# Modulation weights at the head of SyncE's queue, small loads on ScalarE, and a one-column root refined on ScalarE

## The chip, the cores and the metric

The kernel runs on one core of a Trainium2 chip. The metric is device time in microseconds (us) of one launch. "Before" is the median of three runs; a separate profiled execution gives the trace.

## What is computed

Two layers (DEPTH = 2) of a backbone over 2048 latent tokens and 256 context tokens, 1024 wide, all in float32. Cut to what matters here:

```
mod_x = silu(c) @ w_ada[l] + b_ada[l]            # shift, scale, gate for the latent tokens
mod_c = silu(c_ctx) @ w_ada[l] + b_ada[l]        # the same for the context tokens
hx = x * rsqrt(mean(x*x) + EPS) * g_pre * (1 + sc_x) + sh_x
px = hx @ w_in[l]                                # columns for four head groups
# mLSTM, Hyena (FFT convolution with a filter made by a small sine MLP), gated linear attention, windowed attention
y = concat(groups) @ w_out[l]
x = x + gt_x * (y * rsqrt(mean(y*y) + EPS) * g_post)
```

The context tokens go the same way with `mod_c`. The filter of the Hyena group is `sin(f1 * (z @ w1 + b1))`, then `sin(f2 * (h @ w2 + b2))`, then a third matrix product.

## The kernel before

Tokens are handled in 18 tiles of 128: two context tiles, then 16 latent tiles. A scheduler of the language orders the instructions of every engine when the program is built, by its own model of durations; each engine then runs its list strictly in that order. All DMA transfers stand in one list, on SyncE (SP).

The start of the program (`start`, L393) does five things that overlap. `ada_prep` (L233) loads 72 short rows (`rows`: the two conditioning vectors, biases, `g_pre`, the sine frequencies), TensorE transposes them, and `fm` and `cs` come out of it. `hy_mlps` (L238 to L1285) is the sine MLP of the filter: per block of up to 512 columns a product (L1265), a scaled copy on ScalarE (`sa`, L1230), five VectorE instructions that reduce the argument (L1231 to L1235), a sine on ScalarE (L1236), and all that once more for the second layer (product at L1271). The sine is in another ScalarE function table than the logarithm and exponential, so a table is loaded ahead of the sines and another after the last one (L1284); the logarithm of every normalisation is tied behind the latter. `ada_first` (L314) loads 16 tiles of the modulation weights, 512 KB each, and multiplies them (L266); from the sums come `A` and `B`, scale and shift per feature. `phase_a` (L382) loads token tiles (`cvhi`, `cvho`, `xh`) and calls `norm_tile` (L349): a Square with a running sum on ScalarE (L360), the inverse root (`rsqrt_mean`), a scaling on VectorE (L364), transposes on TensorE (L370), scale and shift (L374, L377), and a split into a rounded part `hi` (L379) and a remainder `lo`, written `ho` in the rows (L380, GpSimd). Then `weights` (L411) loads and splits the projection weights (`raw`, two buffers; `w`), and the projection itself runs at L480 to L483. Between these runs the rest of the filter (`hy_spectrum`; L1342 to L1350, L1390, L1404).

`rsqrt_mean` (L220) takes a sum of squares `ss` of one column (`nss` in `norm_tile`, `rs` at the end of a layer; 36 and 34 calls) or of four (the head norms; 68 calls). It forms v = mean + EPS on VectorE, Ln and Exp(-0.5 ...) on ScalarE, and one Newton step in three VectorE instructions (L228 to L230).

A layer ends with `tail` (L1605): per tile, the mLSTM chunk (`mlstm_chunk`: decay matrices `E` loaded by L798, L804 to L828 on VectorE, products L810 and L816), the output projection (L1650 to L1652), its norm (L1653 to L1659) and the residual (L1660). Tiles overlap, two or three at a time.

Of the kernel before, what the change touches and what calls it, by code (L numbers as in the profile page):

```python
# [18 lines left out]
P = 128  # L19
D = 1024  # L20
# [136 lines left out]
class Net:  # L157
    def __init__(self, ctx, tc, a):
        self.tc, self.nc, self.a = tc, tc.nc, a
        nc = self.nc  # L160
        pool = lambda name, bufs=1, **kw: ctx.enter_context(tc.tile_pool(name=name, bufs=bufs, **kw))
        nc.scalar.preload_act_table_set("natural_log_exp_and_others")
        self.dram = pool("dram", space=DRAM)
        self.cst = pool("cst")
        self.hp = pool("hp")
        self.wp = pool("wp")
        self.gp = pool("gp")
        self.psp = pool("psp", 2, space=PSUM)
        self.psm = None
        self.nd = 0  # L170
        self.marks, self.pacer = [], None
        self.flip = 0
        self.H2, self.KX, self.KC = {}, {}, None
        self.rev = [1, 0] + list(range(NT - 1, NCT - 1, -1))
        self.ident = self.cst.tile([P, P], F32, name="ident")
        nc.sync.dma_start(out=self.ident, in_=a["c_ident"])
        self.aT = self.dt((NT, P, KD, P), "aT")
# [42 lines left out]
    def rsqrt_mean(self, p, ss, n, tag):  # L220
# [6 lines left out]
        nc.scalar.activation(out=ss, in_=t, func=ACTF.Exp, scale=-0.5)  # L227
        nc.vector.scalar_tensor_tensor(out=t, in0=ss, scalar=-0.5, in1=ss, op0=ALU.mult, op1=ALU.mult)  # L228
# [4 lines left out]
    def ada_prep(self, p):  # L233
        nc, a = self.nc, self.a
        rows = p.tile([64 + 4 * DEPTH, P], F32, name="rows")
        nc.sync.dma_start(out=rows[0:8], in_=a["c"].rearrange("o (k p) -> (o k) p", p=P))
        nc.sync.dma_start(out=rows[8:16], in_=a["c_ctx"].rearrange("(k p) -> k p", p=P))
        for h in range(2):  # L238
            o, c = 64, slice(64 * h, 64 * h + 64)
            nc.sync.dma_start(out=rows[o:o + 2 * DEPTH, c], in_=a["hyena_freq"].rearrange("l j p -> (l j) p"))  # L240
            for j, nm in enumerate(("hyena_b1", "hyena_b2")):
                r = o + (2 + j) * DEPTH
                nc.sync.dma_start(out=rows[r:r + DEPTH, c], in_=a[nm])
        for l in range(DEPTH):
            o = 16 + 24 * l
            nc.sync.dma_start(out=rows[o:o + 16], in_=a["b_ada"][l, :2 * D].rearrange("(k p) -> k p", p=P))
            nc.sync.dma_start(out=rows[o + 16:o + 24], in_=a["g_pre"][l].rearrange("(k p) -> k p", p=P))
# [65 lines left out]

    def ada_first(self):  # L314
        nc = self.nc
        ws = [self.hp.tile([P, 4, D], F32, tag=t, name="ws" + t, bufs=4) for t in ("hi", "ho") * 2]
        slots = [ws[i // 4][:, i % 4] for i in range(16)]

        def load(l, k, u):
            w = slots[u * KD + k]  # L320
            nc.sync.dma_start(out=w, in_=self.a["w_ada"][l, k * P:(k + 1) * P, u * D:u * D + D])
            return [w[:, 256 * q:256 * q + 256] for q in range(4)]
# [70 lines left out]
    def start(self, src):  # L393
        self.pa_banks = ("ab",)
        self.ev = (3,)
        with self.banks("st"):
            with self.pool("ad0", 1) as pa:
                self.ada_prep(pa)
# [839 lines left out]
    def hy_mlps(self, layers, banked=False):  # L1238
        nc, a = self.nc, self.a
        nl = len(layers)  # L1240
        with self.banks("hm") if banked else nullcontext(), self.pool("hm", LG[13]) as p:
# [4 lines left out]
            ls = slice(layers[0], layers[-1] + 1)  # L1246
            for h in range(2):
                r = slice(64 * h, 64 * h + 64)
                nc.sync.dma_start(out=W1[33 * h:33 * h + 33, :, r], in_=a["hyena_w1"][ls].rearrange("l p n -> p l n"))
                nc.sync.dma_start(out=W2[r, :, r], in_=a["hyena_w2"][ls].rearrange("l p n -> p l n"))  # L1250
            zs = {}
            for nm, n in (("x", SEQ // 2), ("c", CTX))[:1 if layers[0] else 2]:
                zs[nm] = p.tile([66, n], F32, name="z" + nm, bufs=1)
                nc.sync.dma_start(out=zs[nm], in_=a["c_z" + nm])
# [494 lines left out]
```

## Time and profile before

| quantity | value |
|---|---|
| median of three runs | 3533.69 us (3526.88 to 3543.3) |
| the profiled execution: its own time | 3536.89 us |
| its span, first to last instruction | 3535.1 us |
| mean granted TensorE clock | 0.944 |
| TensorE (PE) busy | 3226.2 us, 91% |
| VectorE (DVE) busy | 2046.1 us, 58% |
| ScalarE (ACT) busy | 1434.5 us, 41% |
| GpSimd (POOL) busy | 1153.3 us, 33% |

The span is the part of the profiled execution that the trace covers, 1.8 us less than its time. The busy shares are means over stages with different limits, so a stage is read from its own stretch of the trace.

### The profile page before, as it was taken

Reading aid. Unit: us, or ns where it says so; the run is one execution under the profiler, and the core shown is the slowest. Engines: PE = TensorE matmul, PEld = TensorE weight load, DVE = VectorE, ACT = ScalarE, POOL = GpSimd, SP = SyncE. Lnnn points to the kernel's source line nnn. Section 1 sums busy time; section 2 is a strip of 40 time slices with the busy share of each in tenths; the row PEclk is TensorE's granted clock in tenths of the full one; section 3 lists DMA queues with packets and bytes.
Section 4 is the critical chain, followed back from the end, with each engine's and each line's share of the span. In section 5 each row is a group of like instructions: output and inputs, shape, how many; then the busy total and the mean of one; then the engine's idle time right before and its main releaser. Section 6 shows DMA issues by size and latency. Waiting matters only on the chain. (4 is left out here: it accounts for less than half of the span.)

```text
span 3535.1 us, 70724 instructions
## 1 busy us (share of the span) xinstructions
PE 3226.2 (91%) x25897; PEld 2653.8 (75%) x25897; DVE 2046.1 (58%) x5374; ACT 1434.5 (41%) x3722; POOL 1153.3 (33%) x1559
## 2 busy tenths in 40 slices
PE   6989999999998988888998899998999999887998
PEld 4778878798886677777777677776888887776776
DVE  6733565553345565568888534656432457745887
ACT  5513444332544444133444323444333546522433
POOL 3711111233123344145555420112231135422555
PEclk8999999999998989989999899999999999998999
DMA  7374443684355532475444365443863443327453
GB/s 248 105 203 125 116 117 101 186 247 130 111 167 155 149 111 82 120 203 176 154 138 137 97 178 156 118 116 118 242 185 97 123 119 105 101 84 210 152 162 106
DMA packets 554861, 508.24 MB, mean 144 GB/s; under 512 B 114896, under 2 KB 484877, under 8 KB 554515
## 3 DMA queue, kind: packets, MB, share of 16 engines
q1 hardware_dynamic: 554515, 503.73, 48.3%
q8 instruction: 205, 3.36, 0.4%
q14 instruction: 141, 1.16, 0.1%
HBM read 337.64 MB, written 165.92 MB: 142 GB/s over the span
## 5 line engine op out<-in xcount | busy, mean ns | idle before, releaser
L480 PE MATMUL pp<-w,hi 128*128 128x256 f32 (+2 forms) x1984 | 602.8, 305 | 23.6 <-ACT w L425 10.4
L482 PE MATMUL pp<-w,hi 128*128 128x256 f32 (+2 forms) x1984 | 595.6, 301 | 4.5 <-POOL w L426 4.5
L483 PE MATMUL pp<-w,ho 128*128 128x256 f32 (+2 forms) x1984 | 590.8, 298 | 5.1 <-POOL ho L380 5.0
L463 PE MATMUL pp<-hi,w 128*128 128x512 f32 (+1 forms) x1328 | 527.0, 397 | 6.5 <-ACT w L425 5.2
L466 PE MATMUL pp<-hi,w 128*128 128x512 f32 (+1 forms) x1328 | 513.6, 389 | 1.2 <-POOL w L426 1.0
L465 PE MATMUL pp<-ho,w 128*128 128x512 f32 (+1 forms) x1328 | 513.6, 387 | 0.0
L480 PEld LDWEIGHTS pp<-w,hi 128*128 128x128 f32 x1984 | 389.3, 197 | 46.4 <-ACT w L425 13.9
L482 PEld LDWEIGHTS pp<-w,hi 128*128 128x128 f32 x1984 | 390.5, 197 | 17.4 <-issue 8.6
L483 PEld LDWEIGHTS pp<-w,ho 128*128 128x128 f32 x1984 | 391.0, 197 | 16.4 <-issue 7.5
L426 POOL TENSOR_TENSOR w<-raw,w 128x256 fp32r<-128x256 f32 (+2 forms) x256 | 194.1, 775 | 554.0 <-ACT w L425 519.2
L463 PEld LDWEIGHTS pp<-hi,w 128*128 128x128 f32 x1328 | 255.9, 193 | 61.0 <-issue 7.3
L466 PEld LDWEIGHTS pp<-hi,w 128*128 128x128 f32 x1328 | 251.8, 191 | 53.2 <-issue 3.9
L465 PEld LDWEIGHTS pp<-ho,w 128*128 128x128 f32 x1328 | 253.6, 191 | 44.1 <-issue 3.0
L1650 PE MATMUL pp<-woh,w 128*128 128x512 f32 x544 | 235.5, 433 | 19.2 <-ACT pp L1654 9.0
L1651 PE MATMUL pp<-wol,w 128*128 128x512 f32 x544 | 223.4, 411 | 0.0
L1652 PE MATMUL pp<-woh,w 128*128 128x512 f32 x544 | 219.2, 412 | 2.0 <-POOL w L1639 2.0
L1010 ACT COPY M<-X 128x512 f32<-128x512 f32 x204 | 128.9, 632 | 181.5 <-DVE X L1034 73.3
L216 DVE COPY st<-pp 128x256 f32<-128x256 f32 (+2 forms) x152 | 79.6, 524 | 205.2 <-PE pp L483 106.1
L218 ACT COPY st<-pp 128x256 f32<-128x256 f32 (+2 forms) x152 | 68.7, 452 | 262.0 <-PE pp L483 140.9
L1032 DVE TENSOR_TENSOR X<-X,A 128x256 f32<-128x256 f32 x204 | 109.4, 536 | 94.8 <-ACT M L1010 92.6
L425 ACT CAST w<-raw 128x256 fp32r<-128x256 f32 (+2 forms) x256 | 96.9, 407 | 158.1 <-DMA raw<-in_w_in_dram 96.7
L1219 POOL TENSOR_TENSOR sg<-sg,gt 128x256 f32<-128x256 f32 x34 | 24.9, 733 | 393.8 <-ACT sg L654 324.8
(589 smaller groups left out, 6932.2 us busy)
## 6 DMA issues: line engine op xcount, KB each, us to landing
raw<-in_w_in_dram SPq DMA_DIRECT2D x96, 256.0 KB
q<-d_tq SPq DMA_DIRECT2D x68, 256.0 KB
E<-d_mM SPq DMA_DIRECT2D x68, 256.0 KB
d_yraw<-st SPq DMA_DIRECT2D x64, 256.0 KB
raw<-in_w_ada_dram SPq DMA_DIRECT2D x64, 256.0 KB
X<-d_gqk SPq DMA_DIRECT2D x102, 128.0 KB
wsho<-d_aT SPq DMA_DIRECT2D x34, 384.0 KB
kl<-d_tk SPq DMA_DIRECT2D x28, 384.0 KB
```

What stands on the lines that cost most here:

```text
L426: nc.gpsimd.tensor_sub(out=t[:, 1, :n], in0=raw[:, i, :n], in1=t[:, 0, :n])
L463: mm = nc.tensor.matmul(out=ps[:, :n], lhsT=a, rhs=hi[:, k], start=(k == 0), stop=False)
L465: nc.tensor.matmul(out=ps[:, :n], lhsT=a, rhs=lo[:, k], start=False, stop=False)
L466: nc.tensor.matmul(out=ps[:, :n], lhsT=b, rhs=hi[:, k], start=False, stop=(k == KD - 1))
L480: mm = nc.tensor.matmul(out=ps[:, :n], lhsT=a, rhs=wk[k][:, 0, :n], start=(k == 0), stop=False)
L482: nc.tensor.matmul(out=ps[:, :n], lhsT=a, rhs=wk[k][:, 1, :n], start=False, stop=False)
L483: nc.tensor.matmul(out=ps[:, :n], lhsT=b, rhs=wk[k][:, 0, :n], start=False, stop=(k == KD - 1))
L1010: nc.scalar.copy(out=grid(M, 0, (cc, 2), (x, 512 // x), (1, cc)), in_=grid(X, 0, (512 + cc, 2), (x, 512 // x), (1, cc)))
L1032: nc.vector.tensor_mul(out=t, in0=t, in1=grid(A, f + 2 * b + 1, (-2 * b - 1, 2), (2, b), (0, cc)))
L1650: nc.tensor.matmul(out=ps, lhsT=ak[k][:, 0], rhs=hi[:, k], start=(k == order[0]), stop=False)
L1651: nc.tensor.matmul(out=ps, lhsT=ak[k][:, 0], rhs=lo[:, k], start=False, stop=False)
L1652: nc.tensor.matmul(out=ps, lhsT=ak[k][:, 1], rhs=hi[:, k], start=False, stop=(k == order[-1]))
```

## The change

Three edits. (1) The 16 loads of the modulation weights become a function of their own, `ada_load`, called ahead of `ada_prep`. (2) The 18 small loads of `ada_prep` and of layer 0's sine MLP are issued by ScalarE instead of SyncE. (3) Where the root has one column, the Newton step is three ScalarE instructions with one VectorE instruction for -0.5 v, in place of three VectorE instructions.

```
@@ __init__
+        self.half3 = self.cst.tile([P, 1], F32, name="half3")
+        nc.gpsimd.memset(self.half3, 1.5)
@@ rsqrt_mean
         ln = nc.scalar.activation(out=t, in_=v, func=ACTF.Ln)
         nc.scalar.activation(out=ss, in_=t, func=ACTF.Exp, scale=-0.5)
+        if w == 1:
+            nc.vector.tensor_scalar_mul(out=v, in0=v, scalar1=-0.5)
+            nc.scalar.activation(out=t, in_=ss, func=ACTF.Identity, scale=ss)
+            nc.scalar.activation(out=t, in_=t, func=ACTF.Identity, scale=v, bias=self.half3)
+            nc.scalar.activation(out=ss, in_=ss, func=ACTF.Identity, scale=t)
+            return ln
         nc.vector.scalar_tensor_tensor(out=t, in0=ss, scalar=-0.5, in1=ss, op0=ALU.mult, op1=ALU.mult)
@@ ada_prep
-        nc.sync.dma_start(out=rows[0:8], in_=a["c"].rearrange("o (k p) -> (o k) p", p=P))
+        nc.scalar.dma_start(out=rows[0:8], in_=a["c"].rearrange("o (k p) -> (o k) p", p=P))
...
@@ ada_load, ada_first
+    def ada_load(self):
+        ws = [self.hp.tile([P, 4, D], F32, tag=t, name="ws" + t, bufs=4) for t in ("hi", "ho") * 2]
+        self.ada_slots = [ws[i // 4][:, i % 4] for i in range(16)]
+        for i, w in enumerate(self.ada_slots):
+            u, k = i // KD, i % KD
+            self.nc.sync.dma_start(out=w, in_=self.a["w_ada"][0, k * P:(k + 1) * P, u * D:u * D + D])
+
     def ada_first(self):
...
         def load(l, k, u):
-            w = slots[u * KD + k]
-            nc.sync.dma_start(out=w, in_=self.a["w_ada"][l, k * P:(k + 1) * P, u * D:u * D + D])
+            w = self.ada_slots[u * KD + k]
@@ start
             with self.pool("ad0", 1) as pa:
+                self.ada_load()
                 self.ada_prep(pa)
                 self.drain(self.hy_mlps((0,)))
                 self.ada_first()
@@ hy_mlps
+            eng = nc.sync if layers[0] else nc.scalar
-                nc.sync.dma_start(out=W1[33 * h:33 * h + 33, :, r], in_=a["hyena_w1"][ls].rearrange("l p n -> p l n"))
+                eng.dma_start(out=W1[33 * h:33 * h + 33, :, r], in_=a["hyena_w1"][ls].rearrange("l p n -> p l n"))
...
-                nc.sync.dma_start(out=zs[nm], in_=a["c_z" + nm])
+                eng.dma_start(out=zs[nm], in_=a["c_z" + nm])
```

The scheduler orders the rest anew. First place: ScalarE from its first scaled sine argument on, at the start of the program. `sa` and the `h_...` tiles belong to the sine MLP (the two ACT_TABLE_LOAD rows stand ahead of the first sine and behind the last), `mb` to the modulation, `hi...,nss<-cvhi` is the Square of a token tile (the first two are the context tiles), `w<-raw` the rounding of projection weights. In the kernel before:

```order
3 L1230 ACTIVATE sa<-psa,fb,fm 128x512
4 L1230 ACTIVATE sa<-psb,fb,fm 128x512
5 L1236 ACT_TABLE_LOAD
6 L1236 ACTIVATE h_144<-sa 128x512
...
17 L1236 ACTIVATE h_182<-sa 128x256
18 L1284 ACT_TABLE_LOAD
19 L218 COPY mb<-psm 2x256 x2
20 L360 ACTIVATE hi_352,nss<-cvhi 128x8x128 x2
21 L226 ACTIVATE t<-v 128x1
```

The changed kernel, the same place (its line numbers are 10 to 12 higher here):

```order
18 L262 ACTIVATE sg<-fm 128x16
19 L220 COPY mb<-pse 2x256 x2
20 L370 ACTIVATE hi_354,nss<-cvhi 128x8x128
21 L1241 ACTIVATE sa<-psa,fb,fm 128x512
22 L1241 ACTIVATE sa<-psb,fb,fm 128x512
23 L370 ACTIVATE hi_354,nss<-cvhi 128x8x128
24 L370 ACTIVATE hi_422,nss<-cvhi 128x8x128
25 L220 COPY mb<-psm 2x256
26 L436 CAST w<-raw 128x256 x4
27 L220 COPY mb<-psm 2x256
28 L1247 ACT_TABLE_LOAD
...
42 L1296 ACT_TABLE_LOAD
```

A Square of a context tile now stands ahead of the first sine argument, two more Squares and four weight casts ahead of the first sine; in rows 29 to 41, which are left out, stand the sines with five more casts between them.

Second place: SyncE's list in the changed kernel from its start, and then where the loads of the third to the sixth latent tile (`cvho`) stand; `d_H` is the sine MLP's result on its way to memory, `d_tv` and `d_tk` are the first projected tiles.

```order
1 L176 DMA ident<-in_c_ident_dram 128x128
2 L327 DMA wshi<-in_w_ada_dram 128x1024 x4
...
6 L186 DMA tri<-in_c_tri_dram 128x256
7 L186 DMA mbig<-in_c_mbig_dram 128x256
8 L397 DMA cvhi<-in_ctx_dram 128x1024 x2
...
14 L1286 DMA d_H_162<-h_166 128x512
...
33 L1107 DMA d_tv<-mb 128x128 x2
34 L1115 DMA d_tk<-st 2x64x128 x2
35 L397 DMA cvho<-in_x_dram 128x1024 x4
```

In the kernel before, the 18 small loads stand between `ident` and the weights; and `cvho` stands ahead of the first `d_tv`.

Third place: VectorE in the tail of layer 1 around the output norm's root `rs`, before (a stretch that repeats for nine tiles) and after (one tile; the tiles differ):

```order
4603 L225 TENSOR_SCALAR v<-rs 128x1
...
4610 L804 SCALAR_TENSOR_TENSOR E<-E,G,mbig 128x128 x2
4611 L228 SCALAR_TENSOR_TENSOR t<-rs 128x1
4612 L804 SCALAR_TENSOR_TENSOR E<-E,G,mbig 128x128
4613 L229 TENSOR_TENSOR t<-t,v 128x1
4614 L230 SCALAR_TENSOR_TENSOR rs<-t,rs 128x1
4615 L1659 SCALAR_TENSOR_TENSOR wshi<-wshi,rs 128x1024
```

```order
4455 L1669 TENSOR_TENSOR rs<-ss 128x1
4456 L675 TENSOR_TENSOR hh<-hh,ss 128x256
4457 L227 TENSOR_SCALAR v<-rs 128x1
4458 L231 TENSOR_SCALAR v<-v 128x1
4459 L662 TENSOR_SCALAR sg<-og 128x512
4460 L1671 SCALAR_TENSOR_TENSOR wshi<-wshi,rs 128x1024
```

L231 overwrites v, so it comes after ScalarE's Ln has read it; in 9 of the 34 tail tiles it stands directly behind L227 or with one instruction between. Between the start and layer 0's tail, and again between the tails, the lists of TensorE, VectorE and GpSimd stand in the same order as before for long stretches.

## Rows read from the trace of the kernel before

**Rows 1.** Windows: PE, PEld, DVE, ACT, POOL busy (count), TensorE clock, DMA share, GB/s.

```profile
0.00:10.00 10.00, 0.35 (x1) 0.18 (x1) 1.00 (x5) 1.50 (x2) 1.05 (x8) 1.00 0.17 42
30.00:40.00 10.00, 2.57 (x27) 0.78 (x28) 3.48 (x17) 6.47 (x15) 0.00 (x0) 0.80 1.04 396
180.00:190.00 10.00, 5.69 (x21) 4.75 (x22) 2.05 (x3) 1.88 (x4) 0.72 (x1) 0.83 0.67 185
190.00:200.00 10.00, 5.21 (x17) 3.58 (x16) 1.98 (x3) 1.92 (x4) 0.00 (x0) 0.82 0.81 245
```

**Rows 2.** Timeline of SyncE's queue: start, duration, instruction.

```profile
1.20 0.36 SPq L236 DMA_DIRECT2D rows<-in_c_dram  x1
...
8.29 1.77 SPq L321 DMA_DIRECT2D wshi<-in_w_ada_dram  x4
...
26.73 1.61 SPq L387 DMA_DIRECT2D cvhi<-in_ctx_dram  x2
...
57.66 3.84 SPq L387 DMA_DIRECT2D cvho<-in_x_dram  x4
...
70.85 1.25 SPq L1104 DMA_DIRECT2D d_tk<-st  x2
```

**Rows 3.** Timeline of ScalarE, 0 to 75 us; in brackets idle time ahead and its releaser.

```profile
13.32 0.78 ACT L1230 ACTIVATE sa<-psa,fb,fm 128x512 f32<-128x512 f32 x1 [5.62 <-PE psa L1265]
...
31.02 1.28 ACT L1284 ACT_TABLE_LOAD   x1
...
35.85 1.06 ACT L360 ACTIVATE hi<-cvhi 128x1024 fp32r<-128x1024 f32 x1
...
37.95 0.19 ACT L226 ACTIVATE t<-v 128x1 f32<-128x1 f32 x1
...
61.84 1.02 ACT L425 CAST w<-raw 128x256 fp32r<-128x256 f32 x3 [2.23 <-DMA raw<-in_w_in_dram]
...
65.24 0.27 ACT L218 COPY mb<-pp 128x128 f32<-128x128 f32 x1 [0.77 <-PE pp L483]
```

**Rows 4.** Timeline of TensorE, 33 to 75 us.

```profile
33.42 0.61 PE L266 MATMUL psm<-wsho,cs 128*2 128x256 f32 x8 [0.67 <-DMA wsho<-in_w_ada_dram]
...
46.91 0.55 PE L480 MATMUL pp<-w,hi 128*128 128x256 f32 x1
...
64.93 0.28 PE L483 MATMUL pp<-w,ho 128*128 128x256 f32 x1
...
72.20 0.60 PE L370 MATMUL psa<-ident,cvho 128*128 128x128 f32 x4
...
73.07 1.02 PE L1390 MATMUL psd<-kt,C 128*128 128x512 f32 x2
...
74.38 0.49 PE L1349 MATMUL psc<-W,y 64*128 64x512 f32 x1
```

**Rows 5.** Windows of the two tails.

```profile
3400.00:3500.00 100.00, 95.07 (x475) 74.02 (x474) 89.68 (x233) 40.40 (x107) 56.55 (x68) 1.00 0.48 147
1580.00:1740.00 160.00, 144.70 (x673) 115.38 (x673) 141.22 (x342) 64.10 (x179) 92.01 (x96) 0.93 0.52 160
```

**Rows 6.** Instructions of `rsqrt_mean` and L377 by line: durations in ns min/median/max.

```profile
L227 ACT ACTIVATE rs<-t x34: 186/203/204, 1582.3 to 3526.9; 128x1 f32<-128x1 f32 x34
L228 DVE SCALAR_TENSOR_TENSOR t<-rs x34: 132/152/701, 1586.6 to 3527.1; 128x1 f32<-128x1 f32 x34
L377 ACT ACTIVATE cvhi<-psa,B,A x24: 442/457/466, 41.7 to 118.7; 128x128 f32<-128x128 f32 x24
```

**Rows 7.** Timeline of the last tile's root and scaling.

```profile
3526.49 0.15 DVE L225 TENSOR_SCALAR v<-rs 128x1 f32<-128x1 f32 x1
...
3527.73 1.28 DVE L1659 SCALAR_TENSOR_TENSOR wshi<-wshi,rs 128x1024 f32<-128x1024 f32 x1
```

**Rows 8.** Groups by line, VectorE, 1580 to 1900 us: busy us, mean ns.

```profile
L230 DVE SCALAR_TENSOR_TENSOR rs<-t,rs 128x1 f32<-128x1 f32 x18 | 6.7, 372 | 0.3
L228 DVE SCALAR_TENSOR_TENSOR t<-rs 128x1 f32<-128x1 f32 x18 | 5.1, 283 | 3.3 <-ACT rs L227 3.3
```

More of the change, by code (lines that the diff above doesn't have):

```diff
@@ L235, in ada_prep @@
         rows = p.tile([64 + 4 * DEPTH, P], F32, name="rows")
-        nc.sync.dma_start(out=rows[0:8], in_=a["c"].rearrange("o (k p) -> (o k) p", p=P))
-        nc.sync.dma_start(out=rows[8:16], in_=a["c_ctx"].rearrange("(k p) -> k p", p=P))
+        nc.scalar.dma_start(out=rows[0:8], in_=a["c"].rearrange("o (k p) -> (o k) p", p=P))
+        nc.scalar.dma_start(out=rows[8:16], in_=a["c_ctx"].rearrange("(k p) -> k p", p=P))
         for h in range(2):
             o, c = 64, slice(64 * h, 64 * h + 64)
-            nc.sync.dma_start(out=rows[o:o + 2 * DEPTH, c], in_=a["hyena_freq"].rearrange("l j p -> (l j) p"))
+            nc.scalar.dma_start(out=rows[o:o + 2 * DEPTH, c], in_=a["hyena_freq"].rearrange("l j p -> (l j) p"))
             for j, nm in enumerate(("hyena_b1", "hyena_b2")):
                 r = o + (2 + j) * DEPTH
-                nc.sync.dma_start(out=rows[r:r + DEPTH, c], in_=a[nm])
+                nc.scalar.dma_start(out=rows[r:r + DEPTH, c], in_=a[nm])
         for l in range(DEPTH):
             o = 16 + 24 * l
-            nc.sync.dma_start(out=rows[o:o + 16], in_=a["b_ada"][l, :2 * D].rearrange("(k p) -> k p", p=P))
-            nc.sync.dma_start(out=rows[o + 16:o + 24], in_=a["g_pre"][l].rearrange("(k p) -> k p", p=P))
+            nc.scalar.dma_start(out=rows[o:o + 16], in_=a["b_ada"][l, :2 * D].rearrange("(k p) -> k p", p=P))
+            nc.scalar.dma_start(out=rows[o + 16:o + 24], in_=a["g_pre"][l].rearrange("(k p) -> k p", p=P))
         n = 64 + 4 * DEPTH
@@ L312, in ada_gate @@
             nc.sync.dma_start(out=gd[:, 256 * q:256 * q + 256], in_=bg[r])
+    def ada_load(self):
[4 more added lines that the diff above has]
+            self.nc.sync.dma_start(out=w, in_=self.a["w_ada"][0, k * P:(k + 1) * P, u * D:u * D + D])
     def ada_first(self):
-        nc = self.nc
-        ws = [self.hp.tile([P, 4, D], F32, tag=t, name="ws" + t, bufs=4) for t in ("hi", "ho") * 2]
-        slots = [ws[i // 4][:, i % 4] for i in range(16)]
         def load(l, k, u):
-            w = slots[u * KD + k]
-            nc.sync.dma_start(out=w, in_=self.a["w_ada"][l, k * P:(k + 1) * P, u * D:u * D + D])
+            w = self.ada_slots[u * KD + k]
             return [w[:, 256 * q:256 * q + 256] for q in range(4)]
@@ L1246, in hy_mlps @@
             ls = slice(layers[0], layers[-1] + 1)
+            eng = nc.sync if layers[0] else nc.scalar
             for h in range(2):
                 r = slice(64 * h, 64 * h + 64)
-                nc.sync.dma_start(out=W1[33 * h:33 * h + 33, :, r], in_=a["hyena_w1"][ls].rearrange("l p n -> p l n"))
-                nc.sync.dma_start(out=W2[r, :, r], in_=a["hyena_w2"][ls].rearrange("l p n -> p l n"))
+                eng.dma_start(out=W1[33 * h:33 * h + 33, :, r], in_=a["hyena_w1"][ls].rearrange("l p n -> p l n"))
+                eng.dma_start(out=W2[r, :, r], in_=a["hyena_w2"][ls].rearrange("l p n -> p l n"))
             zs = {}
```

## The prediction

> **What bounds the kernel now.** I took TensorE's windows first. It is busy for 91% of the span, so a change pays or costs where TensorE has nothing to do, or where another engine sets the pace of a stage. Two stretches concern this change. The first is the start: in the first 10 us TensorE works for 0.35 us, from 30 to 40 us for 2.57 us [rows 1], and DMA share and bandwidth of the latter say why: the DMA engines run full, at 396 GB/s. The last modulation weight ends TensorE's wait at 33.42 us [rows 4]. The second is the tails, 34 output tiles in all: in layer 1's, VectorE is busy for 89.7 of 100 us and TensorE for 95.1; in layer 0's, 141 and 145 of 160 [rows 5]. Two engines near their limit there, ScalarE at 40%.
>
> **Edits 1 and 2, the start.** SyncE issues the first small load at 1.20 us and the first weight at 8.29 us [rows 2]. With the 18 small loads gone from its list it can issue everything behind them 8.29 - 1.20 = 7.1 us earlier. The bytes don't vanish: the small loads are some 0.42 MB (`zx` and `zc`, 66 x 1280 floats, are 0.34 of it), at 396 GB/s 1.1 us if they come between. So the last weight should land at 26.3 to 27.4 us instead of 33.42.
>
> What that is worth is decided by ScalarE's list. Before, its first sine argument starts at 13.32 us and the table load behind the last sine at 31.02 us [rows 3]: 17.7 us of sine MLP that lay beside the weights' transfer and cost nothing. In the new order a Square of a context tile stands ahead of it, and that tile is loaded behind the 16 weights, `tri` and `mbig`. When does it land? In the trace the Square starts at 35.85 us [rows 3]; by bytes, the three transfers behind the last weight (786 KB at 396 GB/s, 2.0 us) are there at 35.4. Moved by 7.1 us, and up to 1.1 later, that is 28.3 to 29.4 us. I take 28.5. The Square takes 1.06 us, so the first sine argument starts near 29.6 us instead of 13.32: the cover of the sine MLP is gone. From there to the first logarithm it took 37.95 - 13.32 = 24.6 us, of which 5.7 us (32.3 to 37.95) were copies and Squares that now stand inside the chain; leaving them out, 19.0 us: 48.6 us. The chain now also holds two Squares (2.1 us) and nine casts (9 x 0.34 = 3.1 us, from the group of three in [rows 3]); where they fill gaps they are free, at most they add 5.2 us. So the first logarithm comes at 48.6 to 53.8 us; I take 51, since the third and later weight pairs can be loaded only when the first have been read (`raw` has two buffers), which keeps the casts from being all filler. That is **13 us later than 37.95**.
>
> Who waits for it, and what comes back? (a) The projections of the context tiles ended at 64.93 us because the last weights were late: the cast at 61.84 us waited 2.23 us for its load [rows 3, 4]. These casts are now done before the norm, so the projection waits for the norm alone: 51 us, 9 more to the first product (46.91 - 37.95 before [rows 3, 4]), and about 9 for the 48 products of both tiles, at 0.2 us, an estimate from 0.55 us at the low clock and 0.28 at the high one [rows 4], which overlap each other: 69 us, 4 late. (b) The next latent tiles (`cvho`) are the later trouble. Their loads were issued at 57.66 us and their first transpose ran at 72.20 us [rows 2, 4]. They now stand in SyncE's list behind the stores of the first projected tiles, and the last of these was issued 70.85 - 64.93 = 5.9 us behind the projection's end. So the loads go out at about 75 us. A tile of 512 KB takes 1.3 us at 396 GB/s; before, with a full queue, 7.6 us passed from the issue to the ScalarE copy behind which their first Square runs (57.66 to 65.24 [rows 2, 3]); I take 3. From that copy to the transpose it took 7 us. So the transposes come at about 85 us, **13 us late**. (c) TensorE does not idle all that time: three groups of filter products and three filter transforms that came behind this point now come ahead of it. A group is three products of 0.49 us, a transform takes 1.02 us [rows 4]: 3 x (1.47 + 1.02) = 7.5 us. (d) From 180 to 200 us TensorE had 9.1 us without work [rows 1], between a filter transform and its loads; the new order puts projections between these. Anything from 0 to 9 us may return; I take 1, since the filter stage there waits for its own stores and loads. Sum: 13 - 7.5 - 1 = 4.5. With all 9 returned it is -3.5; with nothing returned and the upper end of the chain (2.8 us more) +16. **I take +5 us, bounds -4 and +16.** The third edit's ScalarE work on the 18 tiles of the start lies in this uncertainty.
>
> **Edit 3, the root.** 70 calls: 36 in the token norms, 34 in the tails. Each loses three VectorE instructions and gains one, and ScalarE gains three. On VectorE one takes 152 ns, on ScalarE a one-column instruction 203 ns [rows 6]. The new ones read columns as scale and bias, which no one-column row shows; the nearest: a 128x128 scale and shift takes 457 ns and a copy of that size 270 ns [rows 3, 6], so a column costs about 0.09 us. Three instructions with four columns: 0.61 us at least, 0.97 at most. I take the upper end, since L377 reads just such columns. ScalarE's 70 x 0.97 = 68 us are spread over an engine that is 41% busy; what matters is who waits.
>
> *What the tails may gain.* VectorE saves two instructions: 2 x 0.152 = 0.3 us a tile, 10 us over 34 tiles, if it sets the pace. In layer 0's tail the first and the last of the three take 283 and 372 ns on the mean [rows 8]; with the third taken for the one added, that is 0.66 us, x 18 = 12 us, and with layer 1's 16 x 0.3 = 5 us it is 17 us at most. *What they may lose.* From v to its use took 3527.73 - 3526.49 = 1.24 us in the last tile, where nothing else ran between [rows 7]. The same way is now 1.24 - 3 x 0.152 + 0.97 = 1.75 us, +0.51 (by the lower price +0.15). And v can be scaled only when Ln has read it, so VectorE, which took part in the step before, now waits for ScalarE twice. A tile with no other VectorE work in these places loses 0.51 us, one with enough of it gains 0.3. All 34 losing is +17 us. By the order 9 of 34 are of the first kind: 9 x 0.51 = +4.6; the others 25 x 0.3 = -7.5, of which I let half through, because TensorE at 95% takes over: -3.8. **Sum +1, which I set to 0; bounds -17 and +17.** The four-column head norms are unchanged.
>
> **Sum.** The profiled execution took 3536.9 us; +5 + 0 gives 3542. The median of the runs lies 3.2 us below that execution, so I name 3539 us. About 0.5% (17.7 us) is what a measurement of this kernel tells from no change; my forecast lies inside: **no change that can be told, a little to the slow side.**
>
> **The rivals.**
> *The head start holds.* Everything behind the weights is 7.1 us earlier and the tails gain 10 us: 3536.9 - 17.1 - 3.2 = 3517 us. For it: the 7.1 us are real in SyncE's list, and VectorE is 90% busy in the tail. Against it: the sine MLP's place behind the Square. The Trainium skill (DMA: Bandwidth & Descriptors, section "Issuing engines are not separate DMA queues") says that issuing from two engines saves only the time on the sequencer, as all transfers run on the same 16 engines; by it this rival's start gains the 7.1 us of issue and no more. No row here shows a second issuing engine. Chance 0.15.
> *ScalarE makes VectorE wait in every tail tile.* +17 in the tails with +5 at the start: 3556 us, slower by 0.6%. It decides from (17.7 - 5) / 34 = 0.37 us a tile. For it: only one instruction covers the wait where the place is tight; before, waits for ScalarE at L228 were small (3.3 us in layer 0's tail [rows 8]). Against it: in 25 tiles other VectorE work stands between. The Trainium skill (ScalarE: Activation LUTs, section "Rules for kernel authors") sends multiplications to VectorE, not ScalarE; 152 against 203 ns agree, and by that rule this rival's sign is right. Chance 0.13.
> *The start's delay goes through whole*, +16 us: 3550 us, still within 0.5% unless the tails add 2 us. Chance 0.15, a third of it beyond the bound.
> *The edits cancel within a few us of nothing, for whatever parts*: this is the forecast, 0.57.
>
> **How the numbers follow.** Faster by over 0.5% (below 3516): most of the first rival, 0.12. Slower by over 0.5% (above 3551.4): the second, a third of the third and a little of the forecast's tail, 0.20. Within: 0.68. The range that holds 8 in 10 goes from just above the first rival's time to the second's: 3519 to 3557 us.
>
> **What the profile would show.** Right: the last weight near 27 us; ScalarE idle until a Square near 28.5 us, the first sine argument behind it, the logarithm of the first tile near 51 us; `cvho` transposes well behind 72 us; TensorE less idle around the filter transforms; the tails about as long as before. Wrong: a sine argument ahead of 20 us (then the first rival), the tails shorter or longer by over 12 us, VectorE waiting for L233 or L234's root by over 10 us in all (the second rival), or a stage between the tails, where the order is unchanged, that takes another time than before.

## The result, and the profile after

The changed kernel took 3558.18 us (median of 9 runs, 3543.44 to 3573.51), against 3535.81 us for the kernel before in 9 runs. The ratio is 1.0067, 95% interval [1.004, 1.0094]; a second measurement gave 1.005 [1.0025, 1.0076]. It is slower by about 20 us. I had forecast 3539 us and a range up to 3557. The profiled execution took 3567.15 us, 30 more than the profiled one of before and 9 above the median of its own kernel, so the traces show somewhat more loss than the medians do.

To see where, each matmul of the kernel before was looked up in the other trace (same line, tiles and occurrence), and the difference of the two start times taken; "late at 550 us" is the median of that over the 25 us behind 550 us of the first trace. One pair shows how such a number reads. In the trace of the kernel before (timeline of TensorE):

```profile
550.93 0.88 PE L1211 MATMUL psm<-PT,vl 128*64 128x128 f32 x12
```

and in that of the changed kernel, whose line numbers are 11 higher here:

```profile
580.48 0.88 PE L1222 MATMUL psm<-PT,vl 128*64 128x128 f32 x12
```

TensorE is 29.55 us late. By stage (us gained or lost within each; from 550 to 1150 us all kernels lie within -4 and +5):

| kernel | ratio to before [95%] | start, 0–550 | 1150–1560 | layer 0's tail, 1560–2120 | 2120–3250 | layer 1's tail, 3250–end |
|---|---|---|---|---|---|---|
| before, second trace | – | +0.8 | -0.7 | -0.7 | -0.2 | -1.1 |
| changed | 1.0067 [1.004, 1.0094] | +29.6 | -14.9 | -3.6 | +7.2 | +11.5 |
| changed, again | 1.005 [1.0025, 1.0076] | +30.3 | -14.1 | -0.1 | -0.5 | +12.6 |
| loads_only | 0.999 [0.9978, 1.0001] | +17.2 | -15.4 | -22.1 | +1.9 | +7.2 |
| root_only | 0.9994 [0.9979, 1.0009] | +8.2 | -11.8 | +3.0 | +3.0 | +5.1 |
| weights_first | 0.997 [0.9959, 0.998] | +22.1 | -13.9 | -5.7 | -5.2 | -0.2 |
| weights_first_root | 1.008 [1.0051, 1.0109] | +34.7 | -10.9 | +2.8 | +3.0 | +4.9 |
| root_norms | 1.0007 [0.999, 1.0025] | +29.1 | -14.4 | -21.5 | +0.4 | +10.8 |
| root_tails | 1.0034 [1.0014, 1.0055] | +13.8 | -9.4 | -1.1 | -4.2 | +4.7 |
| before_root_tails | 0.998 [0.9965, 0.9996] | -3.0 | +3.5 | -14.0 | -0.6 | +5.6 |
| root_early | 1.0063 [1.0043, 1.0083] | +26.6 | -12.0 | -4.6 | +1.9 | +14.7 |
| cover | 1.0007 [0.9993, 1.002] | +12.5 | -12.5 | -5.3 | +2.4 | +7.1 |
| cover_loads | 1.0047 [1.0029, 1.0064] | +31.5 | -14.1 | +9.1 | +6.7 | +1.2 |
| cvho_early | 1.0064 [1.0038, 1.009] | +22.3 | -2.3 | -0.4 | +7.5 | +4.7 |
| split_small | 0.9986 [0.9967, 1.0005] | +5.2 | -2.5 | -1.2 | -3.9 | +1.2 |
| null_dma | 1.0028 [1.0007, 1.0049] | +13.6 | -3.9 | +0.9 | +2.3 | -1.0 |
| null_switch | 1.0005 [0.9986, 1.0023] | +6.2 | -13.1 | -3.3 | -0.7 | +12.7 |
| switch_first | 1.0078 [1.0049, 1.0107] | +16.9 | -9.7 | -3.9 | +1.9 | +4.2 |
| split_switch | 0.9969 [0.9954, 0.9985] | -0.8 | -12.3 | +10.6 | -8.1 | +0.5 |

Each row is one profiled execution. Two of one kernel agree within 4 us in every stage but one (the changed kernel's 2120–3250), but these pairs happen to be of nearly equal length, while the executions of one kernel lie up to 30 us apart. *switch_first*'s row is of an execution 15 us below its kernel's median, *root_tails*' 12 below, *loads_only*'s 10 below. A better measure are different kernels whose engines run a stage in the same order, instruction by instruction in the traces. To 250 us the changed kernel and *root_norms* do, at 29.1 to 30.3 us late, and so do *loads_only* and *root_tails*, at 17.2 and 13.8. In layer 1's tail seven traces in the order of before (its own two, null_dma, split_small, split_switch, weights_first, cover_loads) lie within -1.1 and +1.2. From 2120 to 3250 *cvho_early*, in the order of before, shows +7.5, so nothing is read from that column.

**The start, by its steps.** ScalarE in the changed kernel (timeline; ACTq is its DMA issues; [rows 3] before):

```profile
15.54 0.30 ACTq L1266 DMA_DIRECT2D zx<-in_c_zx_dram  x1
18.49 0.30 ACTq L1266 DMA_DIRECT2D zc<-in_c_zc_dram  x1
...
28.77 1.06 ACT L370 ACTIVATE hi<-cvhi 128x1024 fp32r<-128x1024 f32 x1 [1.37 <-DMA cvhi<-in_ctx_dram]
...
29.94 0.78 ACT L1241 ACTIVATE sa<-psa,fb,fm 128x512 f32<-128x512 f32 x1
...
53.93 0.20 ACT L228 ACTIVATE t<-v 128x1 f32<-128x1 f32 x1
...
55.94 0.29 ACT L232 ACTIVATE t<-nss 128x1 f32<-128x1 f32 x1
56.26 1.06 ACT L370 ACTIVATE hi<-cvhi 128x1024 fp32r<-128x1024 f32 x1
...
57.32 0.37 ACT L233 ACTIVATE t<-t,half,v 128x1 f32<-128x1 f32 x1
...
59.13 0.30 ACT L234 ACTIVATE nss<-nss,t 128x1 f32<-128x1 f32 x1
```

The Square came at 28.77 us (forecast 28.5), the first sine argument at 29.94 (29.6), the first logarithm at 53.93 (51). The last rows are the second tile's root: 3.5 us from L232 to the end of L234, since other ScalarE work stands between the three. TensorE ([rows 4] before):

```profile
14.53 0.35 PE L258 MATMUL pse<-ident,rows 72*128 72x72 f32 x1 [14.53 <-DMA rows<-in_g_pre_dram]
...
27.67 1.13 PE L1277 MATMUL psa<-zx,W 66*128 66x512 f32 x2
...
62.41 0.56 PE L491 MATMUL pp<-w,hi 128*128 128x256 f32 x1
...
77.18 0.28 PE L494 MATMUL pp<-w,ho 128*128 128x256 f32 x1
...
96.61 0.60 PE L380 MATMUL psa<-ident,cvho 128*128 128x128 f32 x4
```

The projection of the context tiles began at 62.41 us (forecast 60) and its last product ran at 77.18 (69; 64.93 before). The `cvho` transposes came at 96.61 us, 24 us late where I had 13. SyncE's list ([rows 2] before) shows their loads behind the stores, at 79.51 us (forecast 75), and further on the weights of the query projection, the next one (`raw`, L430):

```profile
74.74 3.37 SPq L1107 DMA_DIRECT2D d_tv<-mb  x2
78.21 1.25 SPq L1115 DMA_DIRECT2D d_tk<-st  x2
79.51 1.93 SPq L397 DMA_DIRECT2D cvho<-in_x_dram  x4
...
210.84 1.39 SPq L430 DMA_DIRECT2D raw<-in_w_in_dram  x1
...
229.31 1.32 SPq L430 DMA_DIRECT2D raw<-in_w_in_dram  x1
```

In the kernel before, loads of the same weights lie among the transforms' loads, for example:

```profile
192.72 1.12 SPq L419 DMA_DIRECT2D raw<-in_w_in_dram  x1
...
202.19 0.93 SPq L419 DMA_DIRECT2D raw<-in_w_in_dram  x2
```

Windows of the kernel before and then of the changed one (columns as in [rows 1]):

```profile
0.00:60.00 60.00, 33.25 (x209) 17.16 (x209) 32.96 (x82) 31.16 (x72) 13.70 (x20) 0.83 0.71 256
60.00:100.00 40.00, 34.49 (x183) 26.47 (x183) 30.59 (x77) 28.36 (x82) 22.59 (x20) 0.87 0.58 194
...
150.00:200.00 50.00, 36.74 (x201) 29.73 (x201) 16.92 (x46) 17.54 (x46) 19.02 (x19) 0.90 0.59 170
200.00:250.00 50.00, 48.22 (x311) 43.41 (x311) 20.10 (x53) 11.58 (x25) 8.77 (x12) 0.93 0.78 207
```

```profile
0.00:60.00 60.00, 20.27 (x153) 8.44 (x153) 23.02 (x60) 24.69 (x53) 8.87 (x19) 0.82 0.70 241
60.00:100.00 40.00, 35.34 (x162) 27.56 (x163) 20.14 (x50) 26.00 (x79) 19.60 (x17) 0.76 0.56 181
...
150.00:200.00 50.00, 38.41 (x228) 32.48 (x226) 28.60 (x66) 27.01 (x78) 23.04 (x17) 0.86 0.52 151
200.00:250.00 50.00, 36.61 (x153) 29.25 (x152) 12.69 (x27) 12.70 (x29) 10.45 (x13) 0.69 0.68 177
...
220.00:230.00 10.00, 6.90 (x16) 4.36 (x16) 2.21 (x4) 2.33 (x4) 0.00 (x0) 0.61 0.73 208
230.00:240.00 10.00, 4.43 (x12) 3.02 (x12) 0.68 (x1) 2.75 (x7) 3.46 (x5) 0.50 0.65 137
```

The first number behind the comma, TensorE's busy time, is what to read: the length of the window minus it is its idle time. The first 100 us lost 12.1 us of busy time, all of it ahead of 60 us, where TensorE has little to do until the first norms are done, and none around `cvho`. The stretch from 200 to 250 lost another 11.6, and there the granted clock is 0.69 in place of 0.93 (in the second traces 0.75 and 0.90). What TensorE waits for from 200 to 250 us in the changed kernel (waits: us in total, times, longest):

```profile
PE pp L491 <- ACT w L436: 5.6, 1, 5.6
PE psc L1416 <- issue: 3.0, 1, 3.0
PE psd L1416 <- DMA t<-in_c_TM_dram: 2.4, 1, 2.4
PE psc L1416 <- DMA t<-in_c_TM_dram: 1.6, 1, 1.6
```

L1416 are the filter's transforms: 16 of them, each with a load of 256 KB, one of 128 KB and a store of 256 KB. In the kernel before, products of the query projection lie between them; here all but one of the loads of its weights come from 229 us on, behind the transforms' transfers. Nothing is left to fill with, and the longest wait is that of the projection's own first product for its rounded weights (`w`).

**The root.** Its three instructions by source line (durations in ns min/median/max; L233 in all 70 calls, the others in the 34 of the tails):

```profile
L232 ACT ACTIVATE t<-rs x34: 278/294/298, 1599.1 to 3556.2; 128x1 f32<-128x1 f32 x34
L233 ACT ACTIVATE t<-t,half,v x70: 368/387/449, 54.7 to 3556.6; 128x1 f32<-128x1 f32 x70
L234 ACT ACTIVATE rs<-rs,t x34: 278/294/296, 1599.8 to 3557.0; 128x1 f32<-128x1 f32 x34
```

Together 0.975 us; my upper price was 0.97. The last tile ([rows 7] before):

```profile
3555.52 0.15 DVE L227 TENSOR_SCALAR v<-rs 128x1 f32<-128x1 f32 x1
...
3557.31 1.28 DVE L1671 SCALAR_TENSOR_TENSOR wshi<-wshi,rs 128x1024 f32<-128x1024 f32 x1 [1.16 <-ACT rs L234]
```

1.79 us from v to its use, where I had 1.75.

### The profile page after: what moved, and what is told of

It reads as the page before. It is cut to its first block, busy times and chain, and to the rows that moved or that the text cites. A ratio compares the mean times of both kernels' runs of the same rounds, so it can differ in the third digit from the quotient of the medians.

```text
span 3565.0 us, 70873 instructions
## 1 busy us (share of the span) xinstructions
PE 3228.1 (91%) x25897; PEld 2666.2 (75%) x25897; DVE 2006.2 (56%) x5234; ACT 1490.9 (42%) x3932; POOL 1160.2 (33%) x1560
## 5 line engine op out<-in xcount | busy, mean ns | idle before, releaser
L491 PE MATMUL pp<-w,hi 128*128 128x256 f32 (+2 forms) x1984 | 605.7, 307 | 29.1 <-ACT w L436 10.3
L493 PEld LDWEIGHTS pp<-w,hi 128*128 128x128 f32 x1984 | 391.1, 197 | 14.4 <-issue 7.3
L1662 PEld LDWEIGHTS pp<-woh,w 128*128 128x128 f32 x544 | 108.0, 198 | 56.2 <-ACT pp L1666 23.9
```

The lines of the kernel that those rows point to most:

```text
L491: mm = nc.tensor.matmul(out=ps[:, :n], lhsT=a, rhs=wk[k][:, 0, :n], start=(k == 0), stop=False)
L493: nc.tensor.matmul(out=ps[:, :n], lhsT=a, rhs=wk[k][:, 1, :n], start=False, stop=False)
L1662: nc.tensor.matmul(out=ps, lhsT=ak[k][:, 0], rhs=hi[:, k], start=(k == order[0]), stop=False)
```

## The experiments

**One edit at a time.** *loads_only* is the changed kernel with the old root, *root_only* the old kernel with the new root.

> The changed kernel without its third edit: weights at the head of SyncE's list, small loads on ScalarE, the root in three VectorE instructions as before. If the start is what costs (theory S: in the trace of the changed kernel TensorE's products run 29.5 us later from 500 to 600 us on, and only a little later by the end), the time is 3555 to 3565 us, 20 to 30 us above the kernel before, and the first logarithm comes near 54 us. If the root on ScalarE is what costs (theory R: VectorE waits in the tails), it is 3530 to 3545 us.

> The kernel before with the third edit alone: one-column roots refined on ScalarE, all loads as before. Theory S: within 10 us of the kernel before, 3526 to 3545 us, and the first logarithm near 38 us as before. Theory R: 3550 us or more, with the gain in time lost between 1600 and 2000 us and after 3250 us.

In *loads_only* the first logarithm comes at 53.9 us and the `cvho` transposes at 86.1, though its `cvho` loads stand ahead of the first stores, which begin at 77.08 us:

```profile
73.08 2.69 SPq L389 DMA_DIRECT2D cvho<-in_x_dram  x4
```

Neither theory held: each alone is no slower than before, and together they are. The stage rows show why a sum of edits says little here: the start comes near the sum (17.2 + 8.2, measured 30), but with the loads alone layer 0's tail, which that edit does not touch, was 22.1 us shorter in its new order. A second measurement of the changed kernel confirms the loss, and a second trace of before was taken:

> The changed kernel once more, on the same chip as the two runs below. Loads alone came out at 0.999 and the root alone at 0.9994 of the kernel before, so their sum would be 0.9984, while all three together had been measured at 1.0067. If the edits work on each other through the order of the program (theory A or B, below), the ratio is again 1.004 or more. If the first measurement was a draw (theory C), it is below 1.002.

> The kernel before once more, for a second trace of it. The four traces of changed kernels are all about 12 us faster than it from 1000 to 1450 us, where the order is that of before. If its first trace was a low draw of the clock there (0.84 from 1200 to 1300 us), the second is about 10 us faster in that stretch and this is no gain of any edit; if every edit gains there, the second trace repeats the first within 3 us.

The second trace of before repeats the first within 1.1 us in the stages of the table, so the 9 to 15 us that most kernels gain from 1150 to 1560 us are real. They go with the order: the kernels that keep the old one there (before_root_tails, null_dma) gain nothing like it; *cvho_early* and *split_small*, whose VectorE lists there are 99% alike, both gain 2 us; *root_tails*, *null_switch*, *loads_only* and *weights_first*, 99% alike in another order, 9 to 15. What in the old order is slow was not pursued.

**Where the root costs.** *root_norms* and *root_tails* split the third edit (`if w == 1 and tag == "n":`, and `!=`), the latter also on the loads of before; *root_early* makes -v/2 from the sum of squares.

```
+            nc.vector.tensor_scalar(out=u, in0=ss, scalar1=-0.5 / n, scalar2=-0.5 * EPS, op0=ALU.mult, op1=ALU.add)
...
-            nc.vector.tensor_scalar_mul(out=v, in0=v, scalar1=-0.5)
```

> The changed kernel with the root on ScalarE in the 36 token norms alone; the 34 tails keep three VectorE instructions. Theory A: what the edits cost together lies in the start, where this kernel has the order of the changed one: 1.005 or more, and 25 to 30 us late at 550 us. Theory B: it lies in the tails: below 1.002.

> The changed kernel with the root on ScalarE in the 34 tails alone; the norms keep three VectorE instructions. Theory A: as the loads alone, 0.997 to 1.001, some 17 us late at 550 us. Theory B: 1.004 or more, with the loss after 1600 and after 3250 us.

> The kernel before with the root on ScalarE in the 34 tails alone. The order of all engines is that of before but for the two tails. If the root costs in the tails by itself (theory W), both tails are longer: 5 us or more between 1560 and 2120 us and as much after 3250 us, together 10 to 17 us. If it is worth nothing there (my forecast), the two tails move by less than 5 us each or in opposite ways, and the time is that of before within 6 us. Everything ahead of 1560 us should stay within 3 us of before.

> The changed kernel with -v/2 made from the sum of squares, in a tile of its own, ahead of the logarithm: VectorE has the same number of instructions and waits for ScalarE nowhere between v and the scaling. Theory W (VectorE's wait for the logarithm, and ScalarE's for L231, cost in the tails): 10 us or more come back between 1560 and 2120 us and after 3250 us. Theory O (the tails differ by the order that the program happens to get, not by this wait): the tails move by some amount in either direction, and ScalarE's waits for L231, 13.5 us in layer 0's tail of the changed kernel, go without the time following them.

In the start theory A holds: with the moved loads, the root in the norms is 29.1 us late at 550 us, that in the tails 13.8. In time it does not (1.0007 and 1.0034). In the tails no theory of a fixed price holds. Beside a partner with equal loads and the old root, the new root made layer 0's tail 14 us shorter (before_root_tails), 3 longer (root_only), 8.5 longer (on weights_first) and 21 longer (root_tails against loads_only). What a tail takes goes with its order. In layer 1's tail the seven traces in the order of before, all with the old root, lie within -1.1 and +1.2 us. Seven kernels share another order (at least 98% alike) with the root on ScalarE, and lie at +4.2 to +7.1. *loads_only*, *root_norms* and *null_switch* share a third order with the old root, and lie at +7.2 to +12.7, where the changed kernel's +11.5 and +12.6 lie too. In layer 0's tail *cover_loads* and *split_switch* share an order with the old root, at +9.1 and +10.6. So the changed kernel's loss in layer 1's tail can't be put down to its root.

Nor is it ScalarE's wait: it waited 17.7 us in all for L231, root_early takes that away, and both tails stay within 5 us of the changed kernel's. In its place VectorE now waits for ScalarE to have read `u` (who waited for it, us and times):

```profile
  DVE u L230: 5.8, 6
```

VectorE's wait for the finished root, the sign that I named for the second rival, root_early does not take away: 12.6 us in the changed kernel, 15.0 in root_early. It doesn't make the tails long either: *before_root_tails*, the second line, waits 16.2 us and is 0.2% faster than before.

```profile
  DVE wshi L1671: 12.6, 16
```

```profile
  DVE wshi L1667: 16.2, 19
```

**The weights first, all on SyncE.**

> The first edit alone: the weights' loads stand at the head of SyncE's list, and the 18 small loads stand behind them on SyncE too; the root as before. In its order one sine argument stands ahead of the first Square, the sines behind three Squares. Theory S: the small rows land behind the weights, near 27 us, so the sine arguments and the weights' products both start near 28 us, the first logarithm comes near 52 us or later, and the time is 3550 to 3570 us. If what costs is that ScalarE issues transfers (theory I: its issues stand for 18 us ahead of its first work), this one has none of it and takes 3530 to 3545 us.

> The root on ScalarE in norms and tails, on top of the kernel with the weights' loads first, which measured 0.997. If the root costs time wherever the loads have been moved (20 us on top of the loads alone, as the changed kernel shows), this is near 1.003 to 1.005. If the sum in the changed kernel was an accident of its order, it is 0.995 to 0.999.

The start was late by 22.1 us as theory S says (sine argument at 34.4 us, logarithm at 59.6), and yet the kernel is 0.3% faster than before, by stages behind the start; neither theory's time came. With the root on top it is, with *switch_first*, the slowest of all, 12.6 us of that in the start again.

**Is it the order of the start?** *cover* ties ScalarE's Squares and casts behind the last sine and TensorE's weights' products behind the sine products; *cover_loads* is that with the old root; *cvho_early* ties the first stores behind the `cvho` loads. All use the kernel's own order-only dependency, for example:

```
+        self.after(sq, self.sin0, "square after the first sines")
...
+            if T < 2:
+                self.after(sv, self.ld7, "first stores after the cvho loads")
```

> The changed kernel with its start's order tied: on TensorE the three products of the sine MLP's first layer ahead of the weights' products, on ScalarE the Squares and the rounding of weights behind the last sine. Theory S: the first sine argument comes near 21 us, when the small loads of ScalarE's queue have landed, the logarithm near 42 us instead of 54, and 10 to 20 us of the loss come back: 3538 to 3550 us. If the loss lies in the later order (theory L: the cvho loads behind the stores, the filter's transforms among the projections), the logarithm comes early and the time stays at 3553 to 3563 us.

> The kernel with the start's order tied (sine products ahead of the weights' products, Squares and casts behind the sines) and the root as before in VectorE. With the root on ScalarE this order was 12.5 us late at 550 us. If the root's share of the start is 8 us, as root alone showed, it is 3 to 6 us late here; if the root costs only by where cvho stands (theory V), it is 10 us or more late, since cvho stands early in both. The tails have VectorE roots: if the gain of 22 us in layer 0's tail, seen with the loads alone, belongs to VectorE roots in the moved program, it comes again and the time is near 3520 us; if it was an accident of one order, the time is 3535 to 3545 us.

> The changed kernel with one order tied on SyncE: the stores of the two projected context tiles (d_tv, d_tk) behind the loads of the four cvho tiles. Theory V: the first cvho transposes set the start. They ran at 72.2 us before, at 86.1 with the loads alone and at 96.6 and 100.4 in the changed kernel, and TensorE was 17 and 30 us late at 550 us. With the loads ahead of the stores again the transposes come near 86 us and TensorE is 14 to 20 us late at 550 us; the time falls by about 12 us. Theory N: the norms' roots on ScalarE cost this themselves, by their longer way; then TensorE is still 27 us or more late at 550 us, wherever the loads stand.

*cover*'s head stayed late (TensorE, then ScalarE):

```profile
23.23 2.05 PE L1283 MATMUL psa<-zx,W 66*128 66x512 f32 x2 [8.32 <-DMA zx<-in_c_zx_dram]
```

```profile
25.31 0.78 ACT L1247 ACTIVATE sa<-psa,fb,fm 128x512 f32<-128x512 f32 x1 [5.73 <-PE psa L1283]
...
50.79 0.20 ACT L228 ACTIVATE t<-v 128x1 f32<-128x1 f32 x1
```

With the Square out of the way the first sine argument is still at 25.3 us, because `zx` lands at 23.2 (its product ran at 11.2 before). So the order of the start explains 4.6 of the 16.6 us by which the argument was late. *cover*'s time came back to 1.0007 of before all the same: theory S had the time right, but not the early head that was to bring it. And *cover_loads*, with an earlier logarithm (49.4 us) and `cvho` transposes at 84.8, is 31.5 us late at 550 us where *cover*, with the root on ScalarE, is 12.5. So the root's share of the start, 8 us alone and 12 to 13 elsewhere, is no fixed price, and theory V falls as the whole. In *cvho_early* the loads go out at 76.5 us, ahead of the stores, and yet the transposes come at 94.1, not near 86: putting `cvho` back gave 2.5 us there, and 7 to 8 us at 550 us, between the two theories.

**Late landing or late order?** *split_small* shares the small loads between the two engines, ahead of the weights.

```
-        nc.sync.dma_start(out=rows[8:16], in_=a["c_ctx"].rearrange("(k p) -> k p", p=P))
+        nc.scalar.dma_start(out=rows[8:16], in_=a["c_ctx"].rearrange("(k p) -> k p", p=P))
```

> The kernel before with the small loads shared between SyncE and ScalarE and the weights behind SyncE's half, root as before. In its order the sine arguments stand ahead of the Squares, as before. If the small loads land late in the changed kernel because the weights' transfers run beside them (theory T), here they land as early as before or earlier: the transpose of the rows by 7 us, the first sine argument by 14 us, the first logarithm 0 to 4 us ahead of before (38.0 us), TensorE at 550 us between 4 us early and 5 us late. If issuing on ScalarE is slow by itself, the first sine argument comes at 18 us or later.

TensorE, then ScalarE:

```profile
4.96 0.35 PE L250 MATMUL pse<-ident,rows 72*128 72x72 f32 x1 [4.96 <-DMA W<-in_hyena_w_dram]
8.17 2.04 PE L1265 MATMUL psa<-zx,W 66*128 66x512 f32 x2 [2.86 <-DMA zx<-in_c_zx_dram]
```

```profile
10.25 0.78 ACT L1230 ACTIVATE sa<-psa,fb,fm 128x512 f32<-128x512 f32 x1 [4.42 <-PE psa L1265]
...
33.01 0.20 ACT L226 ACTIVATE t<-v 128x1 f32<-128x1 f32 x1
```

Theory T holds: the head is 5 us ahead of before. But at 550 us the kernel is 5.2 us late, just outside what was expected: some 10 us are lost behind the head.

**What a new order costs with no edit.** *null_dma* adds one transfer of 512 bytes, whose tile nothing reads. Behind 550 us all lists stand as before.

```
+        nc.sync.dma_start(out=self.half3, in_=a["c_ident"][:, 0:1])
```

> The kernel before with one more transfer of one column at its head, into a tile that nothing reads. The schedule of the start changes on all engines, and that of everything behind the start stays. The transfer itself is worth about 0.4 us of SyncE's list. Theory O (an order is worth as much as an edit): TensorE at 550 us is 5 us or more away from before, in either direction. If orders are worth little, it is within 3 us. The stages behind 550 us have the order of before and should take its time within 3 us each, also from 1150 to 1450 us, where every kernel in another order was 6 to 16 us shorter.

Theory O holds. The kernel's first logarithm is at 37.5 us and its last transform ends at 221.0 (before 38.0 and 227.1), and yet it is 13.6 us late at 550 us and the kernel 0.28% slower. The stages behind repeat before within 4 us, at another offset. Most of the loss is in the same place as in the changed kernel:

```profile
200.00:250.00 50.00, 42.94 (x185) 34.17 (x185) 13.47 (x29) 9.38 (x20) 6.55 (x9) 0.76 0.69 184
```

The last three runs tie the transforms' loads from the sixth on behind the third weight pair of the query projection, in the changed kernel, in *split_small* and in *null_dma*:

```
+                            for lf in self.ft_loads[5:]:
+                                self.after(lf, lr, "transforms after the next weights")
```

> The changed kernel with one place of SyncE's list tied: the loads of the filter transforms from the sixth on stand behind the load of the third weight pair of the next projection (raw, the query columns), so that this projection's products lie between the transforms, as before. The order ahead of it is the changed kernel's. If the stall from 200 to 250 us is one half of the start's loss (theory M), TensorE is idle there for 3 to 8 us instead of 12 to 13, it is 12 to 20 us late at 550 us instead of 30, and the time falls by 10 to 18 us, to 3543 to 3552. If the transforms' own transfers set the length of that stretch (theory D), the idle time only moves, and TensorE stays 26 us or more late.

> The shared small loads (half on SyncE, half on ScalarE, first logarithm at 33 us, 5 us ahead of before) with the same tie. That kernel was 5 us late at 550 us in spite of its early head, with 15.8 us of idle TensorE from 150 to 200 us and 5.9 from 200 to 250. Theory M: the head start comes through, TensorE is 0 to 6 us early at 550 us. Theory D: it stays 5 us late.

> The kernel before with the one extra transfer at its head and the tie: transforms from the sixth on behind the load of the third weight pair of the query projection. Without the tie it was 13.6 us late at 550 us, with 7.1 us of idle TensorE from 200 to 250 us. Theory M: TensorE's idle time there falls to 1 to 4 us, it is within 5 us of before at 550 us. Theory D (the transforms' transfers set that stretch): still 10 us or more late at 550 us. The stages behind get a new order with the tie, so the whole time may differ from before by 10 us either way; the verdict is the one at 550 us.

The same window in *switch_first*:

```profile
200.00:250.00 50.00, 40.53 (x229) 33.21 (x227) 15.62 (x37) 11.40 (x26) 9.78 (x15) 0.90 0.78 205
```

in *split_switch*:

```profile
200.00:250.00 50.00, 48.27 (x318) 43.84 (x318) 19.61 (x50) 11.41 (x25) 9.23 (x13) 0.97 0.79 215
```

and, with the one ahead of it, in *null_switch*:

```profile
150.00:200.00 50.00, 31.28 (x181) 24.55 (x180) 19.79 (x46) 16.14 (x43) 18.76 (x18) 0.90 0.58 168
200.00:250.00 50.00, 45.81 (x282) 41.00 (x282) 18.44 (x45) 11.42 (x24) 8.69 (x12) 0.90 0.78 203
```

At 550 us 13, 6 and 7 us came back. In *split_switch* that is the idle time of the window, 5.9 us before and 1.7 now. In the other two less idle time went than I expected: 9.5 us of 13.4 stay in *switch_first*, and in *null_switch* it moved to 150–200 us (18.7 in place of 11.4). What came back there is the clock, 0.90 in both in place of 0.69 and 0.76. So theory M holds for the delay at 550 us, in *null_switch* by half, and theory D for much of the idle time. In time, *switch_first* did not gain: the median of 5 runs is 3565.78 us, and its profiled execution (3551 us) is the fastest of them, so that its 13 us at 550 us are one execution's and not shown for the kernel. Nor does either of the other two differ in time from its partner beyond the intervals. *split_switch*, at 0.9969 [0.9954, 0.9985], beats both kernels, and has neither the root nor the weights at the head.

## Why the prediction was wrong

- **Edits 1 and 2, the head: right to 3 us, for a part of the reason.** The Square, the sine argument and the logarithm came where forecast. I put the lost cover down to the Square alone. *cover* shows a second reason that I had priced at 1.1 us: the small loads, issued beside the weights, land late (rows transposed at 14.53 us, before 6.8). Of the 12 us by which *cover*'s `zx` product was late, 8.5 were its late issue (15.86 us, before 7.33) and 3.5 a longer way from there. The Trainium skill (DMA: Bandwidth & Descriptors, "Issuing engines are not separate DMA queues") says that transfers from all engines interleave on the same DMA engines; the traces agree (in the first 25 us SyncE's packets took 87.7% of the 16 engines' time and ScalarE's 6.2%). Here that went with a cost: 18 issues took ScalarE until 18.8 us, against 7.1 us on SyncE before [rows 2].
- **(a) and (b) were too small.** The context tiles' projection ended 12 us late where I had 4: filter products and transposes stand between its products (68.55 to 72.92 us), and it began 2.4 us behind forecast. `cvho` was 24 us late where I had 13. The loads alone gave nearly my figure (86.1 us, forecast 85), but by luck: my reason was that the `cvho` loads stand behind the first stores, and there they stand ahead of them. I had left the third edit's work on the 18 first tiles "in this uncertainty"; it is worth 8 us alone and 12 to 13 on top of the moved loads, in the orders that these kernels got. The first tile's root took the 0.5 us more that I worked out, the second's 3.5 us, because ScalarE's other work stands between its instructions.
- **What comes back, (c) and (d), is the step that failed.** I took 7.5 and 1 us off. With the loads alone, whose transposes came where forecast, TensorE is 17.2 us late at 550 us and not 4.5: nothing came back. (c) looked at the wrong gap: in the changed kernel TensorE lost 13.0 us of busy time ahead of 60 us, and none from 60 to 100, where the moved filter work was to fill. For (d) I wrote of the idle time around the transforms that "anything from 0 to 9 us may return". From 150 to 200 us 1.7 us did, but from 200 to 250 it rose from 1.8 to 13.4 us at a lower clock. I asked which waits the new order would fill, and not which filling it would take away. My bounds were -4 and +16, the traces show +30. The rival that came nearest in the start is the third, the delay going through whole; the stall added about as much again. The first, the head start, fell with the first sine argument.
- **Edit 3 in the tails: within its bounds, not by its arithmetic.** Price and chain were right to 0.04 us. The tails moved by -3.6 and +11.5, but the same root gave -14 to +21 in layer 0's tail by the order around it. The rival of VectorE waiting gave nearly the measured time (3556 us), and its sign came: VectorE waited 12.6 us for the root in 16 places, over the 10 that I named. But it puts 17 us in the tails and 5 in the start, where the traces show 8 to 12.5 and 30, and *before_root_tails* waits 16.2 us and is faster than before. So its time is near by luck.
- **What no step held:** -15 us from 1150 to 1560 us, where neither a one-column root nor a moved load lies. Without it the loss in the traces would be half as large again. It stays open why, beyond the new order.

The change does lose time in the start: both of its traces show it, and the loads and the root each do alone. How much of the 20 us belongs to the edits and how much to the order they happened to get stays open: *null_dma*, with no edit, lost 13.6 us there, and *cover*, with all three edits and another order, is as fast as before.

## What to carry over

Where a scheduler orders the program, price an edit's own instructions, and then look in the new order for the stage that waits for transfers and ask what still fills it: that stage lost about as much here as the head did. Ask of bulk loads at the head what they share the DMA engines with: here the small loads that start the sine MLP's chain landed 12 us later beside them. Before a difference of half a per cent is put down to an edit, time a kernel with a meaningless edit that moves the order: here that alone was 0.28%. And compare stages between kernels that run them in the same order: that tells an edit from an order.

## What was unexpected of the hardware

ScalarE's issue of 18 small loads beside the weights took 18 us, with pauses of 2.0 to 2.7 us between groups, and its first computation (18.84 us) stood behind all of them; ahead of the weights *split_small*'s 10 took 5.2 us. TensorE's clock in the changed kernel was at its lower level (0.50, 1.2 GHz) from 230 to 240 us, after a window with 6.90 us of work in 10; with more products between the transforms the mean was 0.90 and above. A one-column ScalarE instruction takes 203 ns [rows 6], 294 with a column as scale, 387 with columns as scale and bias.
